# A hybrid decoder on one core: how the bias table is written, which engine copies the queries, and a new order of the mixers' parts

## The chip, the core and the metric

The kernel runs on one core of a Trainium2 chip. The core has five engines that work side by side, each through its own queue in order: TensorE (PE, matrix products and transposes), VectorE (DVE), ScalarE (ACT), GpSimd (POOL) and SyncE (SP), which issues the DMA transfers. The metric is the device time of one execution in microseconds (us); less is better.

## What is computed

The reference runs a sequence of 512 tokens with 1024 features through two layers, in float32. A layer is

```
x = LN(alpha*x + mixer(x))
x = LN(alpha*x + square(relu(x @ w_up)) @ w_down)
x = x + sigmoid(x @ w_gate + b_gate) * (p[i] @ w_proj)
```

The first layer's mixer (the even one) has two halves. Eight heads do latent attention: queries and keys are multiplied out of normalized low-rank inputs, with a rotary part. Eight more heads do attention in a sliding window of 128 tokens, with two key and value heads and a learned sink for each head; to the scores of a head h is added a bias that depends only on the distance of query and key, `rel_bias[bucket(distance), h]`. The second layer's mixer (the odd one) has 16 heads of causal attention in which the running sum of a forget gate's logarithm is added to the scores. Each mixer ends in one output projection.

## The kernel before, in words

**Arithmetic.** Every matrix operand is held as a high and a low part (`hi`, rounded by ScalarE, and `lo`, the rest, subtracted by VectorE or GpSimd), and a product is three matrix products (`mm3`, line 515: high by high, high by low, low by high). All of these are issued at line 512, whatever their stage. The helper `split` (line 500) makes a pair; `tt` (line 486) is the subtraction of weights and MLP operands; `transposes` (line 520) turns tiles on TensorE.

**Stages.** `start` loads x and the first weights and multiplies the sliding-window keys and two query pairs. Then come the even mixer, its output projection with a layer norm for each of four blocks of 128 tokens, the MLP (seven groups of products with fewer multiplications, then one plain group), a second layer norm and the gated embedding; then the same for the second layer with the odd mixer.

**Order.** The program first lists all operations, and a planner (`Plan`, line 254) then puts them into one order for each engine. It knows an estimated duration for each operation and a priority, which is the operation's place in the list plus a shift. It goes through time, and whenever an engine is free it gives it, of the operations that are ready and whose buffers are free, the one with the lowest priority number. Operations marked `port` (line 374) are kept apart in this plan: all of GpSimd's and those of VectorE with the mark, one at a time. On the chip nothing of this is left but the order; each engine takes its instructions in that order, and waits where an input is late.

**The mixers' parts.** The strings `EVEN` and `ODD` (lines 51 to 58) list the parts of the two mixers, each with the shift of its operations. In `EVEN`, `bias` builds the bias table, `q1` and `q3` are query projections, `kv` and `qn` the latents of a block, `s0` to `s7` the sliding-window heads, `m0` to `m7` the latent heads with their projections `mk` and `mq`. In `ODD`, `Q`, `K` and `V` are projections, `G` the forget gates, `F0` to `F15` the heads, `O` the splits of their outputs. Weight loads have the shift of the part that asked for them.

**The bias table.** `e_bias` (line 838) multiplies the 32 bias rows with a one-hot matrix on TensorE (line 844): the result has for each head 384 distances. VectorE copies it to SBUF (`e`, line 846). One transfer (line 847) writes the eight rows of `e`, each 32 times, to a DRAM scratch. A pair of heads then reads its tile `T` back with one element of offset from row to row in four transfers (line 1070), which wait on SyncE for the write. VectorE adds T to the scores and takes their minimum (line 659).

**The stacks of queries.** For a pair of heads, `q_stack` (line 745) takes the projected queries from a PSUM bank and makes for each head a tile `q2`, whose two halves of 64 rows both hold the high part, and a tile `qlo` with the low part in one half. ScalarE rounds the high part out of the bank (line 752), VectorE subtracts for the low part (line 753), and VectorE copies the high part to the other half (line 755). GpSimd clears the unused half of `qlo` early on. There are four query parts in the even mixer and eight in the odd one, two heads each.

**Softmax of a head.** VectorE adds bias or mask (line 659), ScalarE takes the exponential (line 664), VectorE the reciprocal (line 670), GpSimd multiplies (line 673), TensorE transposes, ScalarE and VectorE split, TensorE multiplies with the values.

**Layer norm.** `layer_norm` (line 1210) has two passes of VectorE over each half of the features (lines 1220 and 1222); four transposes and a split follow for each half. `gate` (line 1387) is the gated embedding's last step.

Of the kernel before, what the change touches and what calls it, by code (L numbers as in the profile page):

```python
# [29 lines left out]
F = mybir.dt.float32  # L30
# [4 lines left out]
ALU = mybir.AluOpType  # L35

P = 128
S = 512
# [9 lines left out]
        (5, 10, ((0, 1, 2), (3, 4, 5), (6, 7))),  # L48
        (10, 16, ((0, 1), (2, 3), (4, 5), (6, 7))))

EVEN = ("q1-40 bias+484 kv0+288 kv1-172 qn0+452 kv2-28 kv3-116 rk-132 qn1-532 qn2+352 qn3-24 s0+164 s1+328 "
        "ckv-476 c+76 q3-40 s2-444 s3-16 v0-56 s4+212 s5+192 cq-312 v1-12 s6-24 v2+24 v3+192 os0-444 r-32 s7+68 "
        "mk0+224 mq0-140 m0-124 m1+192 mk1-28 mq1-144 os3+536 os2+192 m2+168 m3-28 mk2-108 mq2-568 om0+248 m4+4 "
        "os1+628 m5-20 mk3-576 om2+116 mq3-188 m6-144 m7-192 om3+144 om1-484").split()
ODD = ("Q0+88 V0+24 V1-84 V2+64 V3-380 V4-40 V5+68 V6+72 V7+12 G+32 V8-48 V9+100 V10+44 K0-32 K3+24 F0+172 Q4-20 "
       "Q1+52 K1+108 F2-68 V11-180 F1+68 Q2+72 K2+100 F4-48 F5-68 K4+80 F3-68 Q3+96 F6-32 F7+16 F8 K7-28 F9-80 "
       "Q5+8 K5-160 F10-52 Q6+128 F11-40 K6+100 F12-80 Q7+100 F13-8 O4-88 O3+188 F14-112 O0+88 F15-40 O5+108 "
       "O6-32 O2-160 O1-32 O7+124").split()
EVEN_Q = 2
START = "x0 002 x1 104 x2 024 204 048 x3 x5 x4 x6 148 x7 248".split()  # L60
WARM = 8
# [151 lines left out]
def layout(I):  # L213

    I = {k: np.asarray(v) for k, v in I.items()}
    A = {}
    A["wall"] = np.concatenate([np.ascontiguousarray(f(I)).reshape(-1) for _, f, _ in weight_pieces()])
    A["xT0"] = np.ascontiguousarray(I["x"][0].T.reshape(KD, P, S))
    A["xn"] = np.ascontiguousarray(I["x"][0])
    A["pT"] = np.ascontiguousarray(I["p"][:, 0].transpose(0, 2, 1).reshape(2, 2, P, S))  # L220
    rb = np.zeros((P, P), I["rel_bias"].dtype)
    rb[:32, :8] = I["rel_bias"]
    rb[32, :8] = 1.0
    A["relb"] = rb
# [207 lines left out]
class Trunk:  # L432
# [312 lines left out]
    def q_stack(self, bank):  # L745

        out = []
        for e_ in range(2):
            rs, ot = slice(64 * e_, 64 * e_ + 64), slice(64 - 64 * e_, 128 - 64 * e_)
            q2, lo = self.u("q2", R), self.u("qlo", R)  # L750
            self.pool(0.53, lambda e, lo=lo, ot=ot: e.memset(lo[ot, :].bitcast(F), 0.0), [], [(lo, 1)])
            self.act(S, lambda e, q2=q2, rs=rs: e.copy(q2[rs, :], bank[rs, :]), [bank], [(q2, 0)], True)
            self.dve(S, lambda e, q2=q2, lo=lo, rs=rs: e.tensor_tensor(lo[rs, :], bank[rs, :], q2[rs, :].bitcast(F), ALU.subtract),  # L753
                     [bank, (q2, 0)], [(lo, 0)])
            self.dve(S, lambda e, q2=q2, rs=rs, ot=ot: e.tensor_copy(q2[ot, :], q2[rs, :].bitcast(F)), [(q2, 0)], [(q2, 1)],  # L755
                     dur=0.34)
# [81 lines left out]
    def e_bias(self):  # L838
# [5 lines left out]
        self.pe(4 * t_pe(384), lambda: [nc.tensor.matmul(pe[:, :384], rb[:], oh[:], start=True, stop=True)], [rb, oh], [pe])  # L844
        et = self.u("e", F, (P, 384))
        self.dve(384, lambda e: e.tensor_copy(et[:], pe[:, :384]), [pe], [et])
        self.dma(4e5, lambda: (self.scratch["e"].rearrange("(h r w) -> h r w", h=8, r=32),
                               et[0:8, :].unsqueeze(1).broadcast_to([8, 32, 384])), [et], [self.dram["e"]])
        self.sinks = self.load("sm16", (P, 8), lambda: A["sinks"].broadcast_to([P, 8]), "sinks")
        self.nsinks = self.p.buf("sm16", (P, 8), F, "nsinks")  # L850
        self.dve(8, lambda e: e.tensor_scalar(self.nsinks[:], self.sinks[:], -1.0, None, ALU.mult), [self.sinks], [self.nsinks])
# [358 lines left out]
    def layer_norm(self, x, g, b):  # L1210
# [7 lines left out]
        self.rsqrt(lambda: rv[:, 1:2], lambda: rv[:, 0:1], [(rv, 0)], (rv, 1))  # L1218
        for h in range(2):
            self.dve(S + 57, lambda e, h=h: e.scalar_tensor_tensor(x[h][:], x[h][:], mv[:, 0:1], g[h][:], ALU.subtract, ALU.mult),  # L1220
                     [mv, g[h]], [x[h]])
            self.dve(S + 57, lambda e, h=h: e.scalar_tensor_tensor(x[h][:], x[h][:], rv[:, 1:2], b[h][:], ALU.mult, ALU.add),  # L1222
                     [(rv, 1), b[h]], [x[h]])

    def out_proj(self, x, order, after):
        xh, xl = self.X
# [160 lines left out]
    def gate(self, ws, h, tb, c, n, q, xx, bg):  # L1387
# [89 lines left out]
```

## Time and profile before

| | us |
|---|---|
| median of 3 runs | 1292.09 |
| lowest and highest of them | 1290.82, 1293.58 |
| the profiled execution | 1293.08 |
| its span, first to last instruction | 1291.3 |
| TensorE busy in the span | 1241.7 (96%) |
| VectorE busy | 1034.0 (80%) |
| ScalarE busy | 604.0 (47%) |
| GpSimd busy | 509.0 (39%) |

The profile comes from one execution; what lies between its time and its span is 1.8 us around the first and the last instruction. A shares-of-busy row is an average over stages that differ: the two mixers take about 160 us and 240 us with all engines at work, the MLP stages are long and regular. Matrix products overlap in their pipeline, so a busy TensorE is one that has no gap, not one at its peak. Its clock has two levels, 2.4 GHz (a granted clock of 1.00) and 1.2 GHz (0.50). A wait is named by what ended it.

### The profile page before, as it was taken

How to read it: one execution, taken by the hardware profiler on the slowest of the kernel's cores; microseconds unless marked ns; L12 is line 12 of the kernel's file. 1: busy time of each engine (PE TensorE's matmuls, PEld its weight loads, DVE VectorE, ACT ScalarE, POOL GpSimd, SP SyncE). 2: the span in 40 equal slices, each digit the busy share in tenths (PEclk: the TensorE clock that was granted, in tenths of full speed). 3: DMA queues.
4: the chain of work that ended last, by engine and by line, in shares of the span. 5: the costliest groups of instructions: out<-in, count | busy, mean ns of one | idle time of the engine just before them, and what ended most of it. 6: DMA issues, size and time to landing. Idle time of an engine off the chain costs nothing. (4 is left out here: it accounts for less than half of the span.)

```text
span 1291.3 us, 17294 instructions
## 1 busy us (share of the span) xinstructions
PE 1241.7 (96%) x6108; PEld 1043.7 (81%) x6108; DVE 1034.0 (80%) x1871; ACT 604.0 (47%) x1156; POOL 509.0 (39%) x408
## 2 busy tenths in 40 slices
PE   9798899999999999999999999998999999999998
PEld 6786787878888888878888888787788888888877
DVE  6379779899989898595544877978999999997774
ACT  6358772444444445333343777723444344444231
POOL 3255333354545543312122557321554545453110
PEclk9899999999999999999999999999999999999999
DMA  6331433233223322413332422441223332242131
GB/s 208 90 110 52 148 116 114 66 103 115 85 95 105 123 86 79 154 50 114 113 102 84 130 90 91 164 147 50 95 68 119 110 117 96 82 131 83 64 114 49
DMA packets 46782, 132.82 MB, mean 103 GB/s; under 512 B 5976, under 2 KB 8664, under 8 KB 46696
## 3 DMA queue, kind: packets, MB, share of 16 engines
q1 hardware_dynamic: 46696, 131.72, 31.3%
q8 instruction: 48, 0.79, 0.2%
q14 instruction: 38, 0.31, 0.1%
HBM read 126.03 MB, written 4.62 MB: 101 GB/s over the span
## 5 line engine op out<-in xcount | busy, mean ns | idle before, releaser
L488 POOL TENSOR_TENSOR wl<-raw,wh 128x1024 fp32r<-128x1024 f32 (+4 forms) x78 | 182.3, 2337 | 433.2 <-ACT wh L551 395.8
L551 ACT CAST wh<-raw 128x1024 fp32r<-128x1024 f32 (+5 forms) x150 | 152.6, 1021 | 202.7 <-DMA raw<-in_wall_dram 108.4
L488 POOL TENSOR_TENSOR wf<-raw,wf 128x512 fp32r<-128x512 f32 x84 | 129.1, 1557 | 142.9 <-ACT wf L584 132.7
L512 PE MATMUL mm<-xh,wh 128*128 128x512 f32 (+1 forms) x416 | 162.1, 390 | 2.2 <-DVE k L767 0.8
L512 PE MATMUL mm<-xl,wh 128*128 128x512 f32 (+1 forms) x416 | 159.6, 384 | 0.8 <-DVE xl L503 0.7
L512 PE MATMUL mm<-xh,wl 128*128 128x512 f32 (+1 forms) x416 | 159.3, 383 | 0.0
L488 DVE TENSOR_TENSOR wl<-raw,wh 128x1024 fp32r<-128x1024 f32 (+4 forms) x72 | 97.0, 1347 | 36.0 <-ACT wh L551 33.7
L584 ACT CAST wf<-raw 128x512 fp32r<-128x512 f32 x168 | 96.7, 619 | 33.2 <-PE t L512 17.8
L512 PE MATMUL t<-wf,rh 128*128 128x512 f32 x336 | 103.8, 390 | 0.4 <-ACT wh L551 0.4
L673 POOL TENSOR_SCALAR t<-t,st 128x256 f32<-128x256 f32 (+3 forms) x128 | 68.4, 554 | 87.7 <-DVE st L670 65.8
L512 PEld LDWEIGHTS mm<-xh,wh 128*128 128x128 f32 x416 | 78.9, 190 | 17.9 <-ACT xh L502 1.4
L512 PE MATMUL mm<-wh,xh 128*128 128x384 f32 (+5 forms) x232 | 84.8, 365 | 7.9 <-DVE qlo L753 2.9
L512 PEld LDWEIGHTS mm<-xl,wh 128*128 128x128 f32 x416 | 78.8, 190 | 15.6 <-DVE xl L503 2.0
L488 DVE TENSOR_TENSOR wf<-raw,wf 128x512 fp32r<-128x512 f32 x84 | 91.3, 1100 | 0.0
L512 PEld LDWEIGHTS mm<-xh,wl 128*128 128x128 f32 x416 | 78.6, 189 | 15.6 <-DVE wl L503 0.4
L512 PE MATMUL mm<-wh,xl 128*128 128x384 f32 (+5 forms) x232 | 82.0, 354 | 0.0
L512 PE MATMUL mm<-wl,xh 128*128 128x384 f32 (+5 forms) x232 | 81.9, 353 | 0.0
L664 ACT ACTIVATE t<-t,st 128x256 f32<-128x256 f32 (+3 forms) x128 | 68.6, 538 | 25.2 <-DVE st L659 24.4
L512 PEld LDWEIGHTS t<-wf,rh 128*128 128x128 f32 x336 | 62.8, 188 | 14.4 <-ACT wh L551 0.8
L512 PE MATMUL s<-wf,rh 128*128 128x512 f32 x224 | 69.2, 390 | 2.6 <-ACT rh L502 2.6
L502 ACT CAST rh<-s 128x512 fp32r<-128x512 f32 x56 | 33.3, 618 | 73.9 <-DVE s L488 73.8
L1332 DVE TENSOR_TENSOR x<-x,t 128x512 f32<-128x512 f32 x100 | 64.8, 676 | 1.4 <-PE t L512 1.3
(295 smaller groups left out, 3296.6 us busy)
## 6 DMA issues: line engine op xcount, KB each, us to landing
raw<-in_wall_dram SPq DMA_DIRECT2D x183, 512.0 KB, 3.3
ck<-scratch_c SPq DMA_DIRECT2D x16, 256.0 KB, 3.8
raw<-in_wall_dram SPq DMA_DIRECT2D x9, 384.0 KB, 3.2
x<-in_xT_dram SPq DMA_DIRECT2D x8, 256.0 KB, 5.5
x<-in_xn_dram SPq DMA_DIRECT2D x8, 256.0 KB, 5.6
g<-in_rows_dram SPq DMA_DIRECT2D x8, 256.0 KB, 4.9
b<-in_rows_dram SPq DMA_DIRECT2D x8, 256.0 KB, 5.3
scratch_x<-x SPq DMA_DIRECT2D x8, 256.0 KB, 2.0
```

The costliest lines, as they stand in the source:

```text
L488: fn = lambda e: e.tensor_tensor(out(), a(), b(), op)
L502: self.act(n, lambda e: e.copy(hi(), src()), r, w, psum)
L512: return [self.nc.tensor.matmul(o(), a(), b(), start=s, stop=e, **kw) for o, a, b, s, e in prods]
L551: self.act(w, lambda e: e.copy(hi[:, :w], raw[:, :w]), [raw], [hi])
L584: self.act(512, lambda e: e.copy(t[:, h[0]], src()), [key], [(t, 0)])
L664: self.act(n, lambda e, i=i, tt=tt: e.activation(tt(), tt(), AF.Exp, bias=nm[:, i:i + 1], scale=-1.0, accum_out=sm[:, i:i + 1]), [(nm, i)] ...
L673: self.pool(0.13 + 1.21e-3 * n, lambda e, i=i, tt=tt: e.tensor_scalar(tt(), tt(), rc[:, i:i + 1], 1.0, ALU.mult, ALU.mult), [rc], [(t, i)])
L1332: self.dve(S, lambda e, b=b, xx=xx: e.tensor_tensor(xx[:], xx[:], b[:], ALU.add), [b], [xx])
```

## The change

It has four parts. The host repeats each head's bias column 16 times, so that the product for the bias table fills 128 rows, and two transfers write 16 of the 32 copies of each head in the scratch each; the scratch holds the same values as before. In `q_stack`, ScalarE copies the high part to the second half too, straight from the PSUM bank; VectorE's copy from the first half goes. The planner's `port` mark is put on more VectorE operations: splits whose source is in SBUF, the two passes of the layer norm and the last two steps of the gate. And the shifts of the mixers' parts are new; the order of the parts in the list, and with it that of the weights in memory, stays.

```diff
-EVEN = ("q1-40 bias+484 kv0+288 kv1-172 qn0+452 kv2-28 kv3-116 rk-132 qn1-532 qn2+352 qn3-24 s0+164 s1+328 "
...
+EVEN = ("q1 bias+484 kv0-292 kv1-60 qn0+452 kv2-296 kv3+64 rk-132 qn1-692 qn2+272 qn3-104 s0+164 s1+292 ckv-156 "
...
-ODD = ("Q0+88 V0+24 V1-84 V2+64 V3-380 V4-40 V5+68 V6+72 V7+12 G+32 V8-48 V9+100 V10+44 K0-32 K3+24 F0+172 Q4-20 "
-       "Q1+52 K1+108 F2-68 V11-180 F1+68 Q2+72 K2+100 F4-48 F5-68 K4+80 F3-68 Q3+96 F6-32 F7+16 F8 K7-28 F9-80 "
...
+ODD = ("Q0+88 V0-104 V1-240 V2+400 V3+1404 V4+1280 V5+2072 V6+1060 V7-1396 G+4 V8-196 V9-156 V10+704 K0-812 "
+       "K3-1684 F0-304 Q4+1704 Q1-880 K1-420 F2+236 V11-1204 F1-1376 Q2-468 K2+360 F4-456 F5+120 K4+1484 F3-644 "
...
     rb = np.zeros((P, P), I["rel_bias"].dtype)
-    rb[:32, :8] = I["rel_bias"]
-    rb[32, :8] = 1.0
+    rb[:32] = np.repeat(I["rel_bias"], P // 8, axis=1)
+    rb[32] = 1.0
...
         if pool:
             self.pool(0.05 + 2.29e-3 * n, sub, r, w)
         else:
-            self.dve(n, sub, r, w)
+            self.dve(n, sub, r, w, port=not psum)
...
             self.act(S, lambda e, q2=q2, rs=rs: e.copy(q2[rs, :], bank[rs, :]), [bank], [(q2, 0)], True)
             self.dve(S, lambda e, q2=q2, lo=lo, rs=rs: e.tensor_tensor(lo[rs, :], bank[rs, :], q2[rs, :].bitcast(F), ALU.subtract),
                      [bank, (q2, 0)], [(lo, 0)])
-            self.dve(S, lambda e, q2=q2, rs=rs, ot=ot: e.tensor_copy(q2[ot, :], q2[rs, :].bitcast(F)), [(q2, 0)], [(q2, 1)],
-                     dur=0.34)
+            self.act(S, lambda e, q2=q2, rs=rs, ot=ot: e.copy(q2[ot, :], bank[rs, :]), [bank], [(q2, 1)], True)
...
         self.dve(384, lambda e: e.tensor_copy(et[:], pe[:, :384]), [pe], [et])
-        self.dma(4e5, lambda: (self.scratch["e"].rearrange("(h r w) -> h r w", h=8, r=32),
-                               et[0:8, :].unsqueeze(1).broadcast_to([8, 32, 384])), [et], [self.dram["e"]])
+        for i in range(2):
+            self.dma(196608, lambda i=i: (self.scratch["e"].rearrange("(h i r w) -> i h r w", h=8, i=2, r=16)[i], et[:]),
+                     [et], [(self.dram["e"], i)])
...
             self.dve(S + 57, lambda e, h=h: e.scalar_tensor_tensor(x[h][:], x[h][:], mv[:, 0:1], g[h][:], ALU.subtract, ALU.mult),
-                     [mv, g[h]], [x[h]])
+                     [mv, g[h]], [x[h]], port=True)
```

The second pass of the layer norm and the gate's last two steps get `port=True` in the same way.

## Rows read from the trace of the kernel before

**Rows 1.** The page's first part: busy time, share of span, instructions.

```profile
PE 1241.7 (96%) x6108; PEld 1043.7 (81%) x6108; DVE 1034.0 (80%) x1871; ACT 604.0 (47%) x1156; POOL 509.0 (39%) x408
```

**Rows 2.** Stretches: length, busy time (instructions) of each engine, clock, DMA share, GB/s.

```profile
20.00:60.00 40.00, 32.42 (x152) 28.76 (x151) 17.56 (x44) 15.10 (x40) 12.10 (x14) 0.87 0.41 105
60.00:160.00 100.00, 89.36 (x516) 77.08 (x515) 79.48 (x213) 72.64 (x181) 45.37 (x59) 1.00 0.31 95
...
205.00:285.00 80.00, 75.01 (x427) 64.04 (x426) 73.95 (x134) 30.60 (x52) 27.87 (x16) 1.00 0.26 86
285.00:560.00 275.00, 275.00 (x1217) 227.53 (x1216) 240.36 (x330) 116.14 (x191) 121.97 (x74) 1.00 0.30 99
...
640.00:840.00 200.00, 191.63 (x1051) 165.69 (x1050) 136.15 (x399) 123.55 (x279) 89.56 (x102) 1.00 0.32 107
...
880.00:940.00 60.00, 54.26 (x328) 47.45 (x328) 53.78 (x87) 24.21 (x44) 22.91 (x14) 0.97 0.26 84
```

**Rows 3.** Timeline of TensorE, 20 to 60: start, length, instruction, idle time before.

```profile
34.92 0.43 PE L512 MATMUL mm<-wh,xh 128*128 128x416 f32 x1 [1.97 <-DVE qlo L753]
...
48.20 0.39 PE L512 MATMUL s<-k,q 128*128 128x256 f32 x1 [3.64 <-DVE st L659]
...
51.40 0.69 PE L512 MATMUL mm<-wh,xh 128*128 128x416 f32 x1 [1.19 <-DVE vsw L503]
```

**Rows 4.** Two stretches at the lower clock, columns as in rows 2.

```profile
49.50:56.30 6.80, 5.61 (x19) 4.98 (x18) 2.89 (x15) 3.02 (x14) 4.49 (x10) 0.50 0.38 110
35.70:39.10 3.40, 3.40 (x12) 3.24 (x11) 0.00 (x0) 0.00 (x0) 0.00 (x0) 0.52 0.57 99
```

**Rows 5.** Timeline of VectorE, 20 to 60.

```profile
28.44 1.80 DVE L755 CAST q<-q 64x512 fp32r<-64x512 f32 x1
...
30.96 1.37 DVE L755 CAST q<-q 64x512 fp32r<-64x512 f32 x1
32.36 0.56 DVE L846 COPY e<-o 128x384 f32<-128x384 f32 x1
...
45.91 0.35 DVE L659 CUSTOM_DVE_ANT_0 t<-s,T,nsinks 128x128 f32<-128x128 f32 x1 [10.68 <-DMA T<-scratch_e]
```

**Rows 6.** Timeline of SyncE's queue, 20 to 60: start, length, issues.

```profile
32.95 0.82 SPq L495 DMA_DIRECT2D scratch_e<-e  x1
...
42.46 1.75 SPq L495 DMA_DIRECT2D T<-scratch_e  x4
44.31 2.23 SPq L495 DMA_DIRECT2D raw<-in_wall_dram  x2
```

**Rows 7.** Two stretches as in rows 2; a DMA group with us to landing.

```profile
37.00:38.00 1.00, 1.00 (x4) 0.95 (x4) 0.00 (x0) 0.00 (x0) 0.00 (x0) 0.50 0.46 52
...
45.00:46.00 1.00, 0.00 (x0) 0.00 (x0) 0.09 (x1) 0.00 (x0) 1.00 (x1) 1.00 0.75 176
...
scratch_x<-x SPq DMA_DIRECT2D x8, 256.0 KB, 2.0
```

**Rows 8.** L755: min/median/max ns; L755, L752: busy us, mean ns; L755, 640:860.

```profile
L755 DVE CAST q<-q x24: 420/494/2464, 26.1 to 828.1; 64x512 fp32r<-64x512 f32 x24
...
L755 DVE CAST q<-q 64x512 fp32r<-64x512 f32 x24 | 19.5, 810 | 0.5
...
L752 ACT CAST q<-mm 64x512 fp32r<-64x512 f32 x22 | 12.8, 582 | 3.3 <-PE mm L512 1.6 <-DVE qlo L753 1.3
...
640.00:860.00 220.00, 13.22 (x16) 1.00 0.35 115
```

**Rows 9.** Chain of waits, 700 to 840, share of the stretch by line.

```profile
by line: PE mm L512 15.3%; ACT t L664 8.9%; PE s L512 8.6%; issue 8.5%; DVE t L659 8.3%; DVE q L755 6.4%; DVE ptl L503 5.1%; ACT wh L551 5.0%; DVE wl L488 4.1%; PE o L512 4.0%; DVE qlo L753 3.4%; DVE k L767 3.2%; ACT pth L502 3.2%; DVE oto 
```

**Rows 10.** First pass of the layer norm: min/median/max ns; busy us, mean ns.

```profile
L1220 DVE SCALAR_TENSOR_TENSOR x<-x,mv,g x32: 730/741/2830, 209.4 to 1237.8; 128x512 f32<-128x512 f32 x32
...
L1220 DVE SCALAR_TENSOR_TENSOR x<-x,mv,g 128x512 f32<-128x512 f32 x32 | 27.9, 871 | 0.0
```

**Rows 11.** One stretch of the even mixer, columns as in rows 2.

```profile
120.00:140.00 20.00, 16.49 (x85) 12.84 (x86) 15.59 (x33) 15.55 (x35) 12.30 (x14) 1.00 0.36 111
```

More of the change, by code (lines that the diff above doesn't have):

```diff
@@ L49 @@
         (10, 16, ((0, 1), (2, 3), (4, 5), (6, 7))))
-EVEN = ("q1-40 bias+484 kv0+288 kv1-172 qn0+452 kv2-28 kv3-116 rk-132 qn1-532 qn2+352 qn3-24 s0+164 s1+328 "
-        "ckv-476 c+76 q3-40 s2-444 s3-16 v0-56 s4+212 s5+192 cq-312 v1-12 s6-24 v2+24 v3+192 os0-444 r-32 s7+68 "
-        "mk0+224 mq0-140 m0-124 m1+192 mk1-28 mq1-144 os3+536 os2+192 m2+168 m3-28 mk2-108 mq2-568 om0+248 m4+4 "
-        "os1+628 m5-20 mk3-576 om2+116 mq3-188 m6-144 m7-192 om3+144 om1-484").split()
-ODD = ("Q0+88 V0+24 V1-84 V2+64 V3-380 V4-40 V5+68 V6+72 V7+12 G+32 V8-48 V9+100 V10+44 K0-32 K3+24 F0+172 Q4-20 "
-       "Q1+52 K1+108 F2-68 V11-180 F1+68 Q2+72 K2+100 F4-48 F5-68 K4+80 F3-68 Q3+96 F6-32 F7+16 F8 K7-28 F9-80 "
-       "Q5+8 K5-160 F10-52 Q6+128 F11-40 K6+100 F12-80 Q7+100 F13-8 O4-88 O3+188 F14-112 O0+88 F15-40 O5+108 "
-       "O6-32 O2-160 O1-32 O7+124").split()
+EVEN = ("q1 bias+484 kv0-292 kv1-60 qn0+452 kv2-296 kv3+64 rk-132 qn1-692 qn2+272 qn3-104 s0+164 s1+292 ckv-156 "
+        "c-204 q3-240 s2-124 s3-36 v0-56 s4+204 s5+224 cq-392 v1-84 s6+8 v2-84 v3-96 os0-204 r-72 s7+56 mk0+784 "
+        "mq0-520 m0-284 m1+104 mk1+132 mq1-104 os3+804 os2-220 m2+132 m3-28 mk2-108 mq2-448 om0-192 m4-156 "
+        "os1+1028 m5-260 mk3-276 om2+36 mq3-188 m6-104 m7-212 om3+144 om1-580").split()
+ODD = ("Q0+88 V0-104 V1-240 V2+400 V3+1404 V4+1280 V5+2072 V6+1060 V7-1396 G+4 V8-196 V9-156 V10+704 K0-812 "
+       "K3-1684 F0-304 Q4+1704 Q1-880 K1-420 F2+236 V11-1204 F1-1376 Q2-468 K2+360 F4-456 F5+120 K4+1484 F3-644 "
+       "Q3+68 F6-1352 F7-384 F8-1156 K7+280 F9-372 Q5+332 K5-184 F10-1236 Q6-1004 F11-172 K6+68 F12-268 Q7+68 "
+       "F13+44 O4-2576 O3+1208 F14-564 O0-532 F15-68 O5-704 O6-492 O2+840 O1-404 O7+2500").split()
 EVEN_Q = 2
@@ L1220, in layer_norm @@
             self.dve(S + 57, lambda e, h=h: e.scalar_tensor_tensor(x[h][:], x[h][:], mv[:, 0:1], g[h][:], ALU.subtract, ALU.mult),
-                     [mv, g[h]], [x[h]])
+                     [mv, g[h]], [x[h]], port=True)
             self.dve(S + 57, lambda e, h=h: e.scalar_tensor_tensor(x[h][:], x[h][:], rv[:, 1:2], b[h][:], ALU.mult, ALU.add),
-                     [(rv, 1), b[h]], [x[h]])
+                     [(rv, 1), b[h]], [x[h]], port=True)
     def out_proj(self, x, order, after):
@@ L1399, in gate @@
         self.act(n, lambda e: e.activation(z[:], z[:], AF.Tanh, scale=0.5), [], [z])
-        self.dve(n, lambda e: e.scalar_tensor_tensor(z[:], z[:], 1.0, q[:, cs], ALU.add, ALU.mult), [q], [z])
-        self.dve(n, lambda e: e.tensor_tensor(xx[:, cs], xx[:, cs], z[:], ALU.add), [z], [(xx, c)] if n < 512 else [xx])
+        self.dve(n, lambda e: e.scalar_tensor_tensor(z[:], z[:], 1.0, q[:, cs], ALU.add, ALU.mult), [q], [z], port=True)
+        self.dve(n, lambda e: e.tensor_tensor(xx[:, cs], xx[:, cs], z[:], ALU.add), [z], [(xx, c)] if n < 512 else [xx], port=True)
     def run(self):
```

## The prediction

> **What bounds the kernel now.** I read the page's busy line first, then a table of stretches, then the waits, timelines and chain inside the stretches that lose time. TensorE is busy for 1241.7 of 1291.3 us [rows 1], so the kernel is bound by TensorE and everything to be won or lost lies in its 49.6 us of idle time and in what it loses at the lower of its two clock levels. The table [rows 2] says where that is. In the MLP stretches TensorE is at 275.00 of 275 us: nothing the change does to VectorE there can show. The idle time is 7.6 us at 20 to 60 and 10.6 us at 60 to 160 (even mixer), 8.4 us at 640 to 840 (odd mixer), and 5.0 and 5.7 us at 205 to 285 and 880 to 940, where layer norms close each mixer. In the even mixer VectorE (79.5 of 100 us) and ScalarE (72.6) are nearly as full as TensorE (89.4), so a delay on either reaches it.
>
> The worst stretch is 20 to 60. TensorE stops three times, each time for VectorE [rows 3]: 1.97 us for a split of the queries (L753), 3.64 us for the bias addition of the first sliding-window head (L659), 1.19 us for a value split queued just behind that. Two pieces of 3.4 and 6.8 us ran at a granted clock of 0.52 and 0.50, the 1.2 GHz level, each right behind these stops [rows 4]; the busy time in them, 3.40 and 5.61 us, would have taken half at 2.4 GHz, a loss of 4.5 us. VectorE itself stood idle 10.68 us until the bias tile T came back from DRAM [rows 5]. The SyncE queue shows why [rows 6]: the table's write is issued at 32.95, the reads of T only at 42.46, because they wait at the queue's head until the write has landed; the next weight loads stand behind them, at 44.31.
>
> **Part 1, the bias table.** The work moved is the same 384 KB, written from 128 rows in two transfers in place of 8 rows in one. While the old write is alone on the queues (37 to 38) the transfers move 52 GB/s with 0.46 of 16 engines busy, 7 GB/s for each busy engine; a moment later, when T is read in shorter runs, it is 176 GB/s at 0.75, 15 GB/s each [rows 7]. Bounds for the new write: the 2.0 us in which 256 KB leave 128 rows for another scratch tensor [rows 7], and the old 8.7 us (33.8 to 42.5). I take 4 us, the old engine count at the rate of the second row (393 KB at 7.4 times 14.7 GB/s is 3.6 us), plus one more issue of about 0.44 us (four T issues in 1.75 us, [rows 6]).
>
> A rule of the Trainium skill ("DMA: Bandwidth & Descriptors", section "Why a DMA increments its semaphore by 16 and not by 1") speaks against this edit: a transfer is spread over as many engines as divide the slowest dimension of both its patterns, and the new target still has 8 heads there. The 0.46 of the lone write, 7.4 of 16 engines, agrees with 8, and by that rule the new write gets no more engines. Another ("SBUF — State Buffer", section "Door 1: The DMA port swizzle") says that rows 0 to 7 reach two of 16 ports, which would make the source rows the brake and the new write several times quicker. No row separates the two; the first is a rival below.
>
> The table also starts earlier, through part 2: the copy of `e` (L846, 32.36) stands behind four query copies on VectorE, of 1.80 and 1.37 us [rows 5] and two of the least length, 0.42 [rows 8], 4.0 us in all. Their replacements on ScalarE can delay the splits between them by up to 4 times 0.58 us [rows 8], so `e` is ready 1.7 to 4.0 us earlier; I take 2.9. Together T is back about 2.9 + (8.7 - 4.4) = 7 us earlier, at 39 in place of 45.9. Of TensorE's time this can return the 3.64 and 1.19 us stops and the 2.8 us lost at the lower clock right behind them: 7.6 us at most. Below, it can return nothing, or cost the extra 0.44 us issue. I take **-6**: the lead of 7 us covers the stops, but the clock may drop somewhere else; the 1.97 us stop I leave where it is.
>
> **Part 2, the query copies.** 24 VectorE copies of 19.5 us in all (median 494 ns, up to 2464) go; 24 ScalarE copies from the bank come, at the 0.58 us of L752, which has the same shape and source: 14.0 us [rows 8]. 13.2 us of the VectorE time lie in the odd mixer, 6.3 in the even one. Queued behind the new copies on ScalarE are the exponentials and the weight rounding; the PSUM bank of the projection is held until the fourth ScalarE copy. In the odd mixer the chain of waits from 700 to 840 has 6.4% of L755, 9.0 us [rows 9]; in its place come copies of 0.58 us on an engine that is also on that chain (the exponentials, L664, have 8.9%). Bounds: the 8.4 us of idle time below, the 16 new copies at 0.58, +9.3, above. I take **-4**, about half of what can be returned. In 60 to 160 the bounds are -10.6 and +4.6 (8 copies); softmax chains that start 7 us earlier give the two full engines slack, but most stops there are short hand-overs that stay, so **-3**.
>
> **Part 3, the planner's port flags.** They add and remove no instruction; the planner now keeps VectorE's SBUF-only operations and GpSimd apart. What such collisions cost shows in the layer norms: L1220 takes 741 ns as a median, 2830 at worst, and 32 of them 27.9 us in place of 23.7 [rows 10]. Bounds: that 4.2 us below; one more collision, +2.1, above. I take **-1**.
>
> **Part 4, the priorities.** They change the order on all five queues in both mixers, SyncE's weight loads and GpSimd's multiplications included, and their effect can't be read off the trace, as the planner still hands a free engine the first ready operation. Below they are bounded by the idle time already counted. Above, by the worst-filled row of a mixer, 120 to 140 with 3.5 us idle in 20 [rows 11]: a whole odd mixer of 200 us like that would idle 35 us, 27 more than now. The row nearest to the new order is the same work in the old one, so I take 0 and keep +27 for the rivals.
>
> **Sum.** -6 - 4 - 3 - 1 = -14 us on the profiled execution's 1293.1 us: 1279.1, forecast **1279**. That execution is 1.0 us above the median shown, 1292.1, so against the median I forecast 13 us, 1.0%. A measurement of this kernel can tell about 0.2%, 2.6 us, from no change: "same" is 1289.5 to 1294.7.
>
> **Rivals.**
> 1. *The write stays slow.* Its engines stay at 7 GB/s each, SyncE's queue still stands some 9 us behind it, and of part 1 only the earlier `e` (2.9 us) counts. Against it speaks the 15 GB/s of the T reads, for it the unchanged 8 heads in the outermost dimension. Then part 1 gives 2 and the stretch at 60 to 160 gives 1; with the odd mixer's 4 and part 3's 1 that is 1293.1 - 8 = 1285.
> 2. *Hidden anyway.* TensorE had projection work for most of VectorE's 10.68 us, so 60 to 160 may only inherit a later version of the same stops; the copies in the odd mixer only change engine. Then the gain is below 2.6 us: about 1291. For it: ScalarE is as full as VectorE in the even mixer. Against: the 3.64 us stop follows T directly.
> 3. *Slower: the odd mixer's tail runs dry.* V3 to V6, Q4 and K4 go back by 1060 to 2072 places while V7, K3 and F1 come forward by 1376 to 1684. If projections are used up, or several heads are left together, TensorE has nothing to put between a head's scores, exponentials, transposes and products. It decides from the point where TensorE's idle time in the odd mixer passes 8.4 + 10 us, the gains of the rest (1293). At the density of rows 11 it idles 35 us: 1293.1 - 10 + 27 = 1310. I price it between the two, at 1301. For it: places that far exceed a part's own length. Against: in the plan no engine idles while an operation for it is ready.
> 4. *More than I take.* The three stops and both half-speed pieces at 20 to 60 go (6.8 + 4.5 us), half of the idle time at 60 to 160 (5.3) and all of the odd mixer's (8.4): -25, 1268.
>
> **How the numbers follow.** Forecast (1274 to 1284) 0.45, rival 1 (1284 to 1289.5) 0.15, rival 2 0.13, rival 3 0.13, rival 4 0.14. Faster by over 0.2% is the forecast, rivals 1 and 4: 0.74; same 0.13; slower 0.13. The range reaches from 1266, a little under rival 4, to 1294, over rival 2; it leaves out rival 3 and a bit of rival 4, under 2 in 10. The three faster cases alone lie in 1266 to 1289.
>
> **What would show it.** Right: reads of T some 4 us behind the table's write, VectorE's wait for T under 5 us, one half-speed piece fewer at 20 to 60, no L755 on VectorE, idle time under 11 us at 20 to 160 and under 6 us at 640 to 840, the MLP stretches unchanged in length. Wrong: a write that still takes 8 us (rival 1), TensorE waiting for L752's second copy or for exponentials behind it, or over 18 us of idle time in the odd mixer (rival 3).

## The result, and the profile after

The changed kernel takes 1275.5 us (median of 4 runs, 1274.6 to 1276.7) against 1292.8 for the kernel before on the same chip: a ratio of 0.986 [0.983, 0.989], 17.3 us faster, where 13 were forecast. The profiled execution has a span of 1272.8 us. The page's busy line:

```profile
PE 1237.7 (97%) x6108; PEld 1044.7 (82%) x6108; DVE 1008.5 (79%) x1847; ACT 615.4 (48%) x1180; POOL 503.2 (40%) x408
```

TensorE is idle for 1272.8 - 1237.7 = 35.1 us in place of 49.6, and its busy time is 4.0 us shorter [rows 1]: 14.5 of the 18.5 us between the spans are idle time. The 24 copies have left VectorE (1871 to 1847 instructions) and joined ScalarE (1156 to 1180). The stretches, at the places of [rows 2]:

```profile
20.00:60.00 40.00, 37.88 (x210) 34.10 (x209) 21.42 (x65) 26.25 (x66) 15.27 (x16) 1.00 0.42 134
60.00:160.00 100.00, 91.16 (x522) 80.73 (x521) 81.60 (x214) 74.70 (x189) 47.75 (x66) 0.97 0.34 107
205.00:285.00 80.00, 75.13 (x422) 64.37 (x421) 71.69 (x130) 33.03 (x58) 31.46 (x19) 0.98 0.21 73
285.00:560.00 275.00, 275.00 (x1221) 227.49 (x1220) 243.92 (x338) 115.85 (x190) 117.84 (x71) 1.00 0.30 99
640.00:840.00 200.00, 194.06 (x1055) 167.36 (x1054) 128.97 (x385) 134.33 (x295) 94.66 (x105) 1.00 0.36 123
```

The idle time at 20 to 60 falls from 7.58 to 2.12 us, and 210 matrix products run there in place of 152. It falls from 10.64 to 8.84 at 60 to 160 and from 8.37 to 5.94 at 640 to 840. The MLP has none, as before. Fixed cuts flatter the odd mixer, whose work stands 9 to 14 us earlier in the changed kernel: from 600 to 845, with TensorE busy at both ends in both kernels, idle time falls from 8.54 to 6.97 only. The whole 14.5 us are then 5.5 at 20 to 60, 1.8 in the rest of the even mixer, 1.6 in the odd one, 2.45 and 1.0 around the two layers' second layer norms (520 to 600, 1170 to 1250), and some 2 in small pieces elsewhere.

Both pieces at 1.2 GHz of [rows 4] are gone, but the even mixer has two new ones:

```profile
64.90:68.50 3.60, 3.60 (x14) 3.60 (x13) 3.21 (x8) 1.86 (x9) 3.59 (x6) 0.53 0.03 3
116.10:119.60 3.50, 3.50 (x13) 2.98 (x13) 3.12 (x10) 2.13 (x8) 1.67 (x5) 0.51 0.49 135
```

Each comes right behind a stop, as before. Two more, of 3.4 us at 232 and 884, stand behind stops of 1.59 us where layer norms close the mixers. These are the two longest stops at 60 to 160 in TensorE's timeline:

```profile
63.69 0.41 PE L512 MATMUL mm<-wh,xh 128*128 128x384 f32 x1 [2.04 <-DVE kl L1060]
...
115.86 0.50 PE L512 MATMUL mm<-ch,wh 128*128 128x512 f32 x1 [3.17 <-DVE ql L503]
```

SyncE's queue, to be held against [rows 6], and VectorE's timeline, against [rows 5]:

```profile
25.48 1.38 SPq L495 DMA_DIRECT2D scratch_e<-e  x2
29.87 1.75 SPq L495 DMA_DIRECT2D T<-scratch_e  x4
32.19 8.41 SPq L495 DMA_DIRECT2D raw<-in_wall_dram  x4
```

```profile
24.91 0.54 DVE L845 COPY e<-o 128x384 f32<-128x384 f32 x1
...
35.76 0.48 DVE L659 CUSTOM_DVE_ANT_0 t<-s,T,nsinks 128x256 f32<-128x256 f32 x1
```

`e` is ready 7.5 us earlier, the reads of T wait 29.87 - 26.86 = 3.0 us for the write to land (8.7 before), and the first bias addition waits for nothing. The copies and the layer norm, against [rows 8, 10]:

```profile
L755 ACT CAST q<-mm x22: 577/582/585, 23.5 to 812.5; 64x512 fp32r<-64x512 f32 x22
...
L1220 DVE SCALAR_TENSOR_TENSOR x<-x,mv,g x32: 735/742/2818, 201.3 to 1220.5; 128x512 f32<-128x512 f32 x32
```

The copy costs 0.58 us each time. The layer norm's pass still has a longest instance of 2.8 us, so the marks did not part VectorE and GpSimd there.

### The profile page after: what moved, and what is told of

Same layout as the page of the kernel before. It is cut to its first block, busy times and chain, and to the rows that moved or that the text cites. A ratio compares the mean times of both kernels' runs of the same rounds, so it can differ in the third digit from the quotient of the medians.

```text
span 1272.8 us, 17267 instructions
## 1 busy us (share of the span) xinstructions
PE 1237.7 (97%) x6108; PEld 1044.7 (82%) x6108; DVE 1008.5 (79%) x1847; ACT 615.4 (48%) x1180; POOL 503.2 (40%) x408
## 4 chain that ended last, share of the span: by engine, by line
PE 78%; DVE 13%; ACT 4%; issue 2%; DMA 2%; POOL 1%; SPq 0%; DVEq 0%; ACTq 0%; POOLq 0%
PE mm L512 30%; PE s L512 20%; PE t L512 15%; PE o L512 10%; PE t L523 2%; DVE wl L488 1%; DMA raw<-in_wall_dram 1%; DVE x L1220 1%; ACT t L664 1%; DVE x L1222 1%; DVE t L659 1%; DVE wf L488 1%; DVE xl L503 1%; DVE rl L503 1%; DVE qlo L753 1%
## 5 line engine op out<-in xcount | busy, mean ns | idle before, releaser
L488 POOL TENSOR_TENSOR wf<-raw,wf 128x512 fp32r<-128x512 f32 x84 | 124.5, 1503 | 128.2 <-ACT wf L584 128.2
L488 DVE TENSOR_TENSOR wl<-raw,wh 128x1024 fp32r<-128x1024 f32 (+4 forms) x72 | 95.7, 1329 | 21.1 <-ACT wh L551 18.4
L488 DVE TENSOR_TENSOR wf<-raw,wf 128x512 fp32r<-128x512 f32 x84 | 100.9, 1220 | 0.0
L512 PE MATMUL t<-wf,rl 128*128 128x512 f32 x168 | 65.4, 389 | 0.0
```

The costliest lines, as they stand in the source:

```text
L488: fn = lambda e: e.tensor_tensor(out(), a(), b(), op)
L512: return [self.nc.tensor.matmul(o(), a(), b(), start=s, stop=e, **kw) for o, a, b, s, e in prods]
```

## The experiments

Twelve kernels, each timed beside the kernel before on the same chip (medians of 1292.5 to 1293.3; differences in the text are taken against the one of the same batch, or against the changed kernel's 1275.5). "Idle" is the profiled execution's span less TensorE's busy time. "Clock" is the time lost at the lower clock level: the span from 0 to 1270 in stretches of 10 us, ten times what each one's granted clock lacks to 1.00, summed. One profiled execution stands behind these two columns; a median stands behind the first. "Clock, all" is the mean over all timed executions of a kernel: the whole span times what its mean granted clock, which is recorded to a thousandth, lacks to 1.000. For the kernel before it is the mean of the 50 executions timed beside the twelve. Their mean clocks reach from 0.987 to 0.997, and a straight line through them gives 0.71 us of time for each us of this loss: the clock moves from one execution to the next, and most of the loss, not all of it, is time.

| kernel | median us | ratio to before [95%] | idle | clock | clock, all |
|---|---|---|---|---|---|
| before | 1292.8 | | 49.6 | 8.6 | 9.0 |
| changed kernel | 1275.5 | 0.986 [0.983, 0.989] | 35.1 | 6.8 | 7.3 |
| *one part on the kernel before* | | | | | |
| d1: new write, old order | 1287.5 | 0.996 [0.994, 0.997] | 44.2 | 1.7 | 5.1 |
| b2: ScalarE copies | 1292.4 | 0.999 [0.998, 1.001] | 46.2 | 11.9 | 9.7 |
| b3: port marks | 1289.6 | 0.997 [0.996, 0.999] | 45.3 | 10.2 | 8.6 |
| b4: new shifts | 1296.8 | 1.003 [1.002, 1.005] | 50.0 | 13.6 | 13.2 |
| j1: every shift moved by 8 | 1291.8 | 0.999 [0.998, 1.001] | 48.4 | 11.9 | 12.2 |
| *one part out of the changed kernel* | | | | | |
| a1: old write, same order | 1277.8 | 0.988 [0.985, 0.990] | 38.8 | 5.1 | 7.0 |
| a4: VectorE copies, same order | 1281.1 | 0.990 [0.987, 0.993] | 41.3 | 10.2 | 6.7 |
| a5: both of these | 1286.9 | 0.995 [0.994, 0.997] | 43.2 | 11.9 | 9.3 |
| c1: no port marks | 1284.4 | 0.993 [0.991, 0.996] | 41.8 | 6.8 | 7.2 |
| c2: old shifts | 1277.8 | 0.989 [0.987, 0.991] | 39.4 | 3.4 | 4.4 |
| *other forms of the write* | | | | | |
| a2: 8 rows spaced by 18 | 1274.5 | 0.985 [0.982, 0.988] | 35.9 | 5.1 | 6.0 |
| a3: 128 rows outermost | 1273.4 | 0.984 [0.981, 0.988] | 38.0 | 3.4 | 4.8 |

**d1, the new write in the old order.** The kernel before with the new bias columns; one planned step issues both transfers, so that every other instruction keeps its place.

```diff
-        self.dma(4e5, lambda: (self.scratch["e"].rearrange("(h r w) -> h r w", h=8, r=32),
-                               et[0:8, :].unsqueeze(1).broadcast_to([8, 32, 384])), [et], [self.dram["e"]])
+        def put():
+            dst = self.scratch["e"].rearrange("(h i r w) -> i h r w", h=8, i=2, r=16)
+            return [self.nc.sync.dma_start(dst[i], et[:]) for i in range(2)]
+        self.op("sp", 0.5, put, [et], [self.dram["e"]], lat=4e5 / 350e3)
```

> The kernel before with every engine's order kept, and the new write in it: 128 rows, two transfers. The query copies stay ahead of the table's copy on VectorE. Theory: T is back 4 to 6 us earlier, the 3.64 us stop of TensorE goes, the stretch at the lower clock behind it may go with it: 1292.8 less 4 to 7, 1286 to 1289. Rival (hidden anyway): within 2 us of 1292.8.

5.0 us faster by the medians (the ratio's interval gives 3.6 to 8.0). The queue, VectorE's first bias addition and the stretch from 20 to 60:

```profile
38.18 1.75 SPq L495 DMA_DIRECT2D T<-scratch_e  x4
```

```profile
41.84 0.35 DVE L659 CUSTOM_DVE_ANT_0 t<-s,T,nsinks 128x128 f32<-128x128 f32 x1 [6.55 <-DMA T<-scratch_e]
```

```profile
20.00:60.00 40.00, 35.91 (x187) 32.58 (x186) 22.22 (x60) 20.09 (x54) 13.98 (x15) 0.96 0.39 115
```

The write alone brings T forward by 4.1 us and takes VectorE's wait from 10.68 to 6.55 us. TensorE's idle time here falls from 7.58 to 4.09: the stop of 3.64 us in [rows 3] is gone, those of 1.97 and 1.19 stay (2.00 and 1.24 here). The 6.8 us piece at the lower clock is gone too. The profiled execution is the fastest of the six (1283.0), so its clock column flatters it. Over all six the loss is 5.1 us, against 8.8 for the kernel before in the same batch; at 0.71 us each, an estimate, these 3.7 us are about half of the gain.

**a1, the old write in the new order.** The changed kernel, with the old bias columns and one transfer of the old form; the step for the second transfer stays in the plan and issues nothing.

```diff
-            self.dma(196608, lambda i=i: (self.scratch["e"].rearrange("(h i r w) -> i h r w", h=8, i=2, r=16)[i], et[:]),
-                     [et], [(self.dram["e"], i)])
+            self.op("sp", 0.5, lambda i=i: put(i), [et], [(self.dram["e"], i)], lat=196608 / 350e3)
```

`put(0)` issues the write of the kernel before, from `et[0:8, :]`.

> The changed kernel with every engine's order kept, but the table written as before: one transfer from 8 rows, each 32 times. Theory (the quick write and the lead it gives pay at 20 to 60): the write takes some 8 us again in place of 3, VectorE waits for T some 5 us more, and the time goes up by 4 to 9 us, to 1280 to 1285. Rival (the new order hides the write anyway, its gain is the priorities'): up by less than 2 us.

2.3 us slower than the changed kernel, between the theory's 4 and the rival's 2. The intervals overlap; what carries the reading is the trace, where every instruction has the same place in its engine's order:

```profile
25.98 0.83 SPq L847 DMA_DIRECT2D scratch_e<-e  x1
35.49 1.76 SPq L495 DMA_DIRECT2D T<-scratch_e  x4
```

```profile
38.93 0.48 DVE L659 CUSTOM_DVE_ANT_0 t<-s,T,nsinks 128x256 f32<-128x256 f32 x1 [2.71 <-DMA T<-scratch_e]
```

```profile
20.00:60.00 40.00, 35.10 (x187) 31.33 (x185) 17.98 (x51) 22.26 (x56) 14.07 (x16) 1.00 0.47 127
```

The old write again takes 8.7 us to land, but VectorE now waits only 2.71 us for T. TensorE's idle time at 20 to 60 goes from 2.12 to 4.90. In the new order the table starts so early that most of the slow write is covered.

**a2, eight rows far apart.** As a1, with the new bias columns, and one transfer from every 18th row in place of eight neighbours. Size, count of transfers, target and pattern stay those of the old write.

```diff
-                                           et[0:8, :].unsqueeze(1).broadcast_to([8, 32, 384]))] if i == 0 else []
+                                           et[0:127:18, :].unsqueeze(1).broadcast_to([8, 32, 384]))] if i == 0 else []
```

> As the run before it (one transfer, 8 source rows, each 32 times, 8 heads outermost in the target), but the 8 source rows stand 18 rows apart in SBUF (0, 18, ..., 126) in place of side by side. If the source rows' places were the brake of the old write: the write takes 3 to 4 us and the time is the changed kernel's, 1275.5, within 2 us. If the number of engines or the repeated reading of 8 rows is the brake: the write takes 8 us and the time is that of the run before it.

1274.5 us: the changed kernel's time. The queue of a2, then a stretch in the midst of the write in a2 and in a1 (last two columns: share of 16 DMA engines, GB/s):

```profile
25.95 0.84 SPq L847 DMA_DIRECT2D scratch_e<-e  x1
29.80 1.83 SPq L495 DMA_DIRECT2D T<-scratch_e  x4
```

```profile
28.00:29.00 1.00, 1.00 (x7) 0.95 (x6) 0.58 (x1) 0.39 (x1) 0.00 (x0) 1.00 0.54 203
```

```profile
30.00:31.00 1.00, 1.00 (x6) 0.84 (x5) 0.54 (x1) 1.00 (x2) 0.32 (x1) 1.00 0.46 52
```

It lands in 3.0 us, as the new write does. The engines are as few as in a1: the busy shares are alike (0.54 and 0.46), and in both the trace has 256 packets of data and 8 of 4 bytes at the transfer's end (its completion packets, below). But at these shares a2 moves 203 GB/s where a1 moves 52. So what made the old write slow is that its eight source rows are neighbours.

**a3, all 128 rows outermost in the target.** The changed kernel with the 16 copies of each head merged with the heads in the target's pattern.

```diff
-            self.dma(196608, lambda i=i: (self.scratch["e"].rearrange("(h i r w) -> i h r w", h=8, i=2, r=16)[i], et[:]),
+            self.dma(196608, lambda i=i: (self.scratch["e"].rearrange("(h r i w) -> i (h r) w", h=8, i=2, r=16)[i], et[:]),
```

> The changed kernel's order and its two transfers from 128 rows, but with a target pattern whose outermost dimension is 128 rows in place of 8 heads (the scratch holds the same). If 8 outermost heads hold the transfer to half of the engines: twice the busy engines, and the reads of T come 0.5 to 1 us earlier; the time stays within 2 us of 1275.5, as VectorE waits less for T now. If not: no difference in the transfers either.

The queue, a stretch in the midst of this write, and the like stretch of the changed kernel:

```profile
25.29 0.81 SPq L495 DMA_DIRECT2D scratch_e<-e  x2
27.75 2.40 SPq L495 DMA_DIRECT2D T<-scratch_e  x4
```

```profile
26.30:27.30 1.00, 0.64 (x3) 0.45 (x3) 0.50 (x2) 0.90 (x2) 0.00 (x0) 1.00 0.94 337
```

```profile
28.00:29.00 1.00, 1.00 (x7) 0.86 (x6) 0.10 (x1) 0.85 (x2) 0.00 (x0) 1.00 0.60 216
```

The busy share goes from 0.60 to 0.94, and the two transfers leave 32 completion packets in place of 16, which fits 16 engines for each in place of 8. (A share is no count of engines: it reaches 1.05 at 12 to 16 in the changed kernel.) The write lands 27.75 - 26.10 = 1.65 us after its last issue in place of 3.0. Its median of 1273.4 is the lowest of all, but its interval overlaps the changed kernel's: with T no longer waited for, a quicker write is worth nothing that these runs can tell.

**b2, the copies on ScalarE alone.** The kernel before with only this line of the change.

```diff
-            self.dve(S, lambda e, q2=q2, rs=rs, ot=ot: e.tensor_copy(q2[ot, :], q2[rs, :].bitcast(F)), [(q2, 0)], [(q2, 1)],
-                     dur=0.34)
+            self.act(S, lambda e, q2=q2, rs=rs, ot=ot: e.copy(q2[ot, :], bank[rs, :]), [bank], [(q2, 1)], True)
```

> The kernel before with the query copies on ScalarE alone (planned anew; old write, marks and priorities). Theory (the copies are worth some 5 us in the odd mixer, and put the table's copy ahead): 1284 to 1288, TensorE's idle time at 640 to 840 from 8.4 to about 6 us. Rival (they need the new priorities): within 2 us of 1292.5.

No change. The mixers in b2, and in the kernel before (at cuts where TensorE is busy in both):

```profile
60.00:180.00 120.00, 108.47 (x621) 95.51 (x621) 92.45 (x254) 88.11 (x223) 55.42 (x78) 0.96 0.31 98
600.00:845.00 245.00, 238.21 (x1282) 204.26 (x1281) 153.47 (x420) 150.69 (x323) 103.33 (x111) 1.00 0.34 113
```

```profile
60.00:180.00 120.00, 109.36 (x642) 95.09 (x641) 96.45 (x260) 89.59 (x224) 54.59 (x75) 1.00 0.31 98
600.00:845.00 245.00, 236.46 (x1281) 203.40 (x1280) 165.56 (x437) 142.51 (x308) 102.55 (x111) 1.00 0.34 112
```

The odd mixer gains 1.75 us of idle time (8.54 to 6.79), as it would by the forecast's kind of reason; but j1 below gains 3.25 us there without touching the copies, so this is not shown to be theirs. The even one loses 0.9 us and falls to a clock of 0.96. Over the profiled execution, the slowest of the ten, idle time goes down by 3.4 us and the loss at the lower clock up by 3.3; over all ten the loss is 9.7 us, up by 1.

b2 also moves the bias table: its write is issued at 28.61 in place of 32.95, and the first reads of T at 38.12, as early as in d1. VectorE still takes up T only at 43.66 (41.84 in d1), and TensorE idles 6.44 us at 20 to 60 (4.09 in d1). An early T is not enough; the order of what stands around it counts too.

**a4, the copies on VectorE in the new order.** The changed kernel; the second copy is issued on VectorE, from the first half, where the plan has it for ScalarE.

```diff
-            self.act(S, lambda e, q2=q2, rs=rs, ot=ot: e.copy(q2[ot, :], bank[rs, :]), [bank], [(q2, 1)], True)
+            self.act(S, lambda e, q2=q2, rs=rs, ot=ot: self.nc.vector.tensor_copy(q2[ot, :], q2[rs, :].bitcast(F)),
+                     [bank], [(q2, 1)], True).emit = "dve"
```

> The changed kernel's order, but each second copy of the queries' high part is done by VectorE from the first half, at the place that the plan has for ScalarE's. Theory (the copies stood in VectorE's way): VectorE has some 20 us more, part of it in collisions with GpSimd, and the time goes up by 3 to 7 us (1279 to 1283), with the table's copy late again. Rival (the copies only change engine): within 2 us of 1275.5, since ScalarE gets back 14 us.

5.6 us slower than the changed kernel, each of the four runs above its highest. The copies by the listing of lines, and the odd mixer in a4 and in the changed kernel:

```profile
L756 DVE CAST q<-q 64x512 fp32r<-64x512 f32 x24 | 17.5, 728 | 10.2 <-ACT q L753 9.9
```

```profile
600.00:845.00 245.00, 235.05 (x1272) 201.43 (x1271) 162.71 (x435) 142.33 (x308) 104.70 (x113) 1.00 0.35 115
```

```profile
600.00:845.00 245.00, 238.03 (x1292) 205.88 (x1291) 153.41 (x425) 150.34 (x322) 104.94 (x112) 1.00 0.35 119
```

VectorE waits 10.2 us ahead of its copies, nearly all of it for ScalarE's first copy, and takes 728 ns for a mean one where ScalarE takes 582. Part of this wait is the experiment's own, as the copies stand at places that were planned for ScalarE. The odd mixer has 9.95 us of idle time in place of 6.97. The bias table's write is issued at 29.22 in place of 25.48, but 2.2 of these 3.7 us were lost ahead of the copies: this execution, the slowest of the four (1284.9), has a piece at the lower clock at 8.6, and ScalarE begins to round the keys at 23.89 in place of 21.67. The copies hold up `e` by 1.5 us, and by as much between a1 and a5 (25.98 and 27.48).

**a5, both old forms in the new order.** a4 with a1's write.

> The changed kernel's order with both the old write and the copies on VectorE. Alone the old write costs 2.3 us and the copies 5.6 us. Theory (the write is worth little only because the table's copy now stands so early that it is hidden; either lead covers for the other): more than their sum, 1285 to 1289, with VectorE waiting for T 5 us or more. Rival (the two are independent): 1283 to 1284.

11.4 us slower than the changed kernel, where 2.3 + 5.6 = 7.9 would be the sum. VectorE's first wait for T, and the stretch from 20 to 60:

```profile
40.62 0.48 DVE L660 CUSTOM_DVE_ANT_0 t<-s,T,nsinks 128x256 f32<-128x256 f32 x1 [3.87 <-DMA T<-scratch_e]
```

```profile
20.00:60.00 40.00, 32.96 (x159) 29.58 (x158) 18.06 (x48) 16.61 (x43) 12.12 (x15) 0.91 0.41 111
```

VectorE waits 3.87 us for T, less than the 5 expected. With the later start and the slow write together, idle time here is 7.04 us, nearly that of the kernel before, and the lower clock is back. In this stretch the two cost more together (4.9 us of idle time) than apart (2.8 and 0.8), as they would if an earlier `e` and a quicker write covered for each other. For the whole kernel that is not shown: idle time grows by 8.1 us, less than 3.7 + 6.2, and the excess of 3.5 us in the medians is small beside ratio intervals that are 4 to 8 us wide.

**b3 and c1, the port marks.** Only the marks on the kernel before (b3), and the changed kernel without them (c1). On the chip a mark is nothing but another order.

```diff
-            self.dve(n, sub, r, w)
+            self.dve(n, sub, r, w, port=not psum)
...
-                     [mv, g[h]], [x[h]])
+                     [mv, g[h]], [x[h]], port=True)
```

For b3:

> The kernel before with the new port marks alone (planned anew). My price was -1 us. Theory: within 3 us of 1292.8, with as many long passes (over 2 us) of the layer norm as before, since the changed kernel still has them. Rival (the marks make the 4 us that the second layer norm of the first layer gained): 1286 to 1289.

For c1:

> The changed kernel without the new port marks (planned anew). The marks alone gave 3 us. If that is theirs and not one plan's luck: 1278 to 1281, with 2 us or more lost again at the second layer norm of the first layer, where every plan with marks lost under 1 us and every plan without them 2 to 5. Rival (luck of a plan): within 2 us of 1275.5 or faster.

The marks bring 2.9 us alone, and taking them out of the changed kernel costs 8.9, over 3 us more than was expected. Where, in c1, stretch by stretch:

```profile
60.00:180.00 120.00, 108.37 (x628) 95.07 (x627) 96.59 (x248) 89.11 (x223) 53.00 (x78) 0.97 0.30 94
...
520.00:600.00 80.00, 78.53 (x361) 64.68 (x360) 57.78 (x109) 26.96 (x39) 16.82 (x9) 1.00 0.28 93
...
1170.00:1250.00 80.00, 77.54 (x355) 63.39 (x354) 57.83 (x110) 25.75 (x37) 14.78 (x6) 1.00 0.30 99
```

and in the changed kernel:

```profile
60.00:180.00 120.00, 111.16 (x642) 98.29 (x640) 94.17 (x247) 87.58 (x221) 54.35 (x78) 0.97 0.30 94
...
520.00:600.00 80.00, 80.00 (x370) 66.15 (x369) 58.61 (x110) 29.47 (x42) 18.03 (x8) 1.00 0.29 98
...
1170.00:1250.00 80.00, 78.57 (x359) 64.35 (x358) 58.46 (x109) 26.28 (x38) 15.06 (x6) 1.00 0.26 87
```

2.79 us more idle time in the even mixer, 1.47 around the first layer's second layer norm, 1.03 around the second layer's. At 520 to 600 all eight kernels with marks have no idle time, and the six without have 1.46 to 2.45 us; at 1170 to 1250 it is 1.43 or 1.44 with marks and 2.44 to 2.47 without. So these two gains, 3.5 us of idle time from the kernel before to b3, are the marks' and not one plan's luck. The 2.79 us in the even mixer may be luck: j1 below loses nearly as much there. Of the 9.6 us between the two profiled spans, 2.9 are longer busy time of TensorE at the same loss of clock, and no run explains them. The timelines of the three engines at that layer norm, first c1 and then the changed kernel, show how:

```profile
571.76 0.66 PE L523 MATMUL t<-ident,x 128*128 128x128 f32 x4 [1.47 <-DVE x L1222]
...
568.83 1.48 DVE L640 SCALAR_TENSOR_TENSOR rv<-nt,rv 128x1 f32<-128x1 f32 x1
...
567.86 2.44 POOL L488 TENSOR_TENSOR wl<-raw,wh 128x1024 fp32r<-128x1024 f32 x1 [5.01 <-ACT wh L551]
```

```profile
568.76 0.60 PE L523 MATMUL t<-ident,x 128*128 128x128 f32 x4
...
564.74 1.48 DVE L640 SCALAR_TENSOR_TENSOR rv<-nt,rv 128x1 f32<-128x1 f32 x1
...
563.76 2.44 POOL L488 TENSOR_TENSOR wl<-raw,wh 128x1024 fp32r<-128x1024 f32 x1 [5.01 <-ACT wh L551]
```

Both have the same collision: beside a GpSimd subtraction of 2.44 us, an operation on one column takes 1.48 us (its like at 562.33 takes 0.14). In c1 TensorE has two groups of gate products in front of the transposes, and then waits 1.47 us. In the changed kernel five groups stand there, from 565.4 on, and it does not wait. The marks do not part the engines here. They make the plan take the two marked passes late, as it keeps them apart from GpSimd's subtraction, and it puts more products in front of the work that VectorE delivers.

**b4 and c2, the shifts.** The kernel before with the new `EVEN` and `ODD` (b4), and the changed kernel with the old ones (c2).

For b4:

> The kernel before with the new priorities alone (planned anew; write, copies and port marks as before). If the priorities carry the gain: 1280 or less. If they are worth something only with the other parts: 1288 to 1300, since they were put on another duration of the write and another place of the copies.

For c2:

> The changed kernel with the old priorities (planned anew; new write, copies and marks). Theory (write and copies carry at least half): 1278 to 1286. Rival (the priorities carry the gain): 1288 or more.

On the kernel before the new shifts cost 4.3 us; with the other three parts they bring 2.3 (all four runs of c2, from 1277.2, lie above the changed kernel's highest, 1276.7). The odd mixer in b4:

```profile
600.00:845.00 245.00, 234.85 (x1247) 201.33 (x1246) 160.95 (x428) 137.52 (x299) 100.94 (x107) 0.99 0.32 106
```

It idles 10.15 us in place of 8.54, yet over the whole execution b4 idles 50.0 us in place of 49.6: what it loses is the clock, 13.6 us in place of 8.6, at seven places from the start to the second layer's first layer norm. All six runs agree: 13.2 us in the mean, where the kernel before lost 8.8 in the same batch. c2 is the reverse: the old shifts idle 4.3 us more than the new ones there, and lose less at the lower clock (4.4 us against 7.3).

**j1, every shift of the kernel before moved by 8, up and down in turn.** A reordering without a purpose, as a measure of a plan's luck.

> The kernel before with each part's shift moved by 8, up and down in turn: how far a plan's luck alone moves the time. If it is small: within 2 us of 1292.5. If it is as large as the gains of the marks or the priorities: 3 us or more either way, and these can't be told from luck.

1291.8 us, no change that can be told in the time. Its stretches:

```profile
60.00:180.00 120.00, 106.92 (x607) 93.24 (x605) 96.09 (x257) 86.18 (x218) 53.27 (x75) 0.96 0.33 100
...
520.00:600.00 80.00, 78.53 (x361) 64.67 (x360) 59.74 (x115) 27.42 (x38) 18.21 (x9) 1.00 0.33 106
600.00:845.00 245.00, 239.71 (x1301) 207.66 (x1300) 161.64 (x440) 142.04 (x308) 105.36 (x112) 1.00 0.34 114
...
1170.00:1250.00 80.00, 77.56 (x354) 63.32 (x354) 61.77 (x114) 27.27 (x38) 18.16 (x8) 1.00 0.28 87
```

The stir is not small inside. The odd mixer idles 5.29 us in place of 8.54, less than in the changed kernel (6.97), the even one 13.08 in place of 10.64, and over all ten runs the lower clock takes 12.2 us in place of 8.7. These happen to cancel in the time. It is one sample and so no bound, but 2 to 3 us of idle time in a mixer, or 3 us at the lower clock, cannot be put down to a part when that part also changes the order. That touches b2, b4, c2 and c1's even mixer. The two stretches around the layer norms are as in the other kernels without marks, and a1, a2, a3, a4, a5 and d1 keep the order.

## Why the prediction was right, and where its steps were not

The time fell by 17.3 us where 13 were forecast, inside the range and on the side with the most chance. The steps fared unequally, and the near sum is in part luck.

- **What bounds it.** Right. Nothing was won in the MLP, and 14.5 of the 18.5 us between the spans are TensorE's idle time, 5.5 of them at 20 to 60.
- **Part 1, -6.** Right in mechanism and nearly in size. d1, with nothing else moved, gives -5.0. The write landed in 3.0 us (4 taken, above the lower bound of 2.0), two issues took 1.38 us (0.82 + 0.44 taken). The term that was mis-sized is the start: `e` was taken 2.9 us earlier, for the copies alone, and came 7.5 earlier. In the changed kernel's order the copies make 1.5 of that (a4, a5), planned anew on the kernel before 4.3 (b2); the rest is the new plan's. With that start the write's own quickness is worth 2.3 us (a1), as the price of a transfer depends on when it begins. The stops of 3.64 and 1.19 us went, as forecast; that of 1.97 went too, which was not.
- **The clock.** The sum took back the loss behind the stops, with the reserve that the clock "may drop somewhere else". It did: the losses are 8.6 us before and 6.8 after, with two pieces at 65 and 116 in place of the two at 36 and 50. Part 1 counted 2.8 us of it as won; over the profiled execution 1.8 stayed won, over all runs 1.7.
- **Part 2, -7.** Nearly right in the final order, wrong for the copies as such. a4 gives 5.6 us, b2 gives nothing. Idle time at 20 to 160 came out at 10.96 (under 11 was named), at 640 to 840 at 5.94 (under 6), the latter by the fixed cuts. By stretch the term was twice too large: it took 3 us at 60 to 160 and 4 in the odd mixer, and 1.8 and 1.6 came back, with all four parts at work. And b2 shows that on the kernel before what the odd mixer gains is given back elsewhere, a case the forecast kept for rival 2.
- **Part 3, -1.** The right sign by the wrong mechanism, and the most mis-sized term: 2.9 us alone, 8.9 when taken out of the changed kernel. It was priced as fewer collisions in the layer norm; the first pass has a longest instance of 2818 ns as before (2830), in 27.9 us in both. What was bought is work placed ahead of late results. Shown for it are the two layer norms: 2.45 us of idle time and 1.0 from the kernel before to the changed one, 1.47 and 1.03 from c1. The rest of the 8.9 us stays open: 2.79 us of idle time in the even mixer, within what a stir of the order moves, and 2.9 us of longer busy time.
- **Part 4, 0.** Off by either measure: +4.3 alone, -2.3 with the others. Alone the loss is mostly the clock's, which the forecast did not have in this term. That shifts are tuned to a plan, and moved to another are no more than a stir, fits both but is not shown. Which mixer's shifts matter wasn't tried.
- **The rivals.** Rival 1, that the write stays slow, was refuted, though its premise held: the engines stayed at 8, and 16 were to be had by another pattern (a3). The "eight engines" were simply not the brake. Rival 2 is b2's story, not the changed kernel's. Rival 3 has its sign, a slower kernel, in b4, but not its mechanism: the odd mixer idles 10.15 us there, far from the 18.4 where it was to decide. Rival 4 has its share at 20 to 60 nearly whole (5.5 of 6.8 us of idle time), and little of the rest: 1.8 of 5.3 us in the even mixer, 2.4 of 8.4 in the odd one at the cuts of [rows 2].

The largest lesson is in the sum. The parts alone on the kernel before bring -5.0, -0.2, -2.9 and +4.3 us, together -4; all at once they bring -17.3. Taken out of the changed kernel one by one they cost 2.3, 5.6, 8.9 and 2.3. The forecast added its terms as if each could be had by itself. What brought it near is in part sound: its terms were bounded by what each stretch had to give back, and the four parts together get most of that at 20 to 60 (5.5 of 7.6 us of idle time, where 6 us were forecast with the clock's share). In part it is luck: the mixers gave half of what was forecast, and the layer norms, priced at 1, gave 3.5.

## What to carry to other kernels

Price a part in the order of instructions in which it will stand, and measure it both ways, alone and taken out: here one part changed its sign between the two, and one went from nothing to 5.6 us. Where a planner orders the work, telling it truly which results come late can be worth as much as making them earlier: 3.5 us of idle time at two layer norms here, beside 2.3 to 5.0 us for the quick write. Count what TensorE loses at its lower clock beside its idle time: removing a stop pays back in full only if no other stop takes over the drop. And measure a stir of the order stretch by stretch before crediting a part with a stretch: j1's total hid 2.4 us lost in one mixer and 3.25 won in the other.

## What the runs showed of the hardware

- **Eight neighbouring source rows are slow by themselves.** The same transfer of 384 KB moves 52 GB/s from rows 0 to 7 and 203 GB/s from eight rows spaced by 18, at busy shares of 0.46 and 0.54 of 16 engines. This agrees with the Trainium skill ("SBUF — State Buffer", section "Door 1: The DMA port swizzle"), by which neighbouring rows share few of the ports.
- **The target's outermost dimension sets how many engines work.** With 8 heads there the busy share is 0.60 and a transfer has 8 completion packets, with 128 rows 0.94 and 16, and the landing goes from 3.0 to 1.65 us. This agrees with the rule of the Trainium skill that the prediction tells ("DMA: Bandwidth & Descriptors", section "Why a DMA increments its semaphore by 16 and not by 1"). The two limits are separate; the first was the one that cost time.
- **A tiny VectorE operation can pay for a whole GpSimd one.** One column takes 1.48 us beside a GpSimd subtraction of 2.44 us, and 0.14 us without; both end at 566.2.
- **The lower clock follows stops, but not every stop.** In the changed kernel both pieces in the even mixer come right behind stops of 2.04 and 3.17 us; c1's stop of 1.47 us at 571.76 has none behind it. The same stop of 1.59 us at the even mixer's closing layer norm has a piece behind it in the changed kernel (at 232) and in a2 (at 231), and none in a3 (the stop ends at 230.34).
